# Five norms between products and a last one: by single token tile, with the next weights split earlier

## The chip, the cores and the metric

One core of one Trainium2 chip. The metric is the device time of one execution in microseconds (us), lower is better. Engines: TensorE (PE, matmuls and transposes), VectorE (DVE), ScalarE (ACT), GpSimd (POOL), and SyncE (SP), whose queue issues the DMAs.

## The reference

512 tokens of width 1024 pass through one block of a first kind and two layers of a second kind, all in 32-bit floating point. The parts between which the change works are chains of a product, a residual add, a norm over the width, and the next product:

```python
# first block
h = h + g1 * (merged @ w_out)
h = h + g2 * swiglu(modulate(rms_norm(h, w), sh2, sc2))     # w_gate, w_up, w_down
h = rms_norm(h, final_norm_w)
# each of two layers; ALPHA = 4 ** 0.25
h = layer_norm(ALPHA * h + g1 * (mix(h) @ w_out), ln1_g, ln1_b)
h = layer_norm(ALPHA * h + g2 * ffn(h), ln2_g, ln2_b)       # ffn: product, 3-tap conv, gate, product
```

`mix` joins three mixers; the third is an attention over three kinds of keys. All modulations (`sh`, `sc`, `g`) come from products of a condition vector with large matrices, which are computed beside the main chain.

## The kernel before, in words

**Products.** A 32-bit product is made of three matmuls on values split in a high and a low part (`mm3`, L389). A weight unit is a raw tile of 128x1024 (`wr`, 3 buffers), loaded on SP's queue (`wload`), multiplied by a gate row on GpSimd where the residual is gated (L370), copied by ScalarE into `wh` and subtracted by VectorE (or GpSimd, argument `e`) into `wl`, 3 buffers each (`feed`, L365). `gemm_R` (L1235) multiplies token tiles with such units: 4 token tiles of 128, two column halves `n` of 512, `nu` units per half, accumulators in PSUM banks by tag; `use` adds the result to the residual rows `x[t][n]`.

**Norms.** `boundary` (L1375) is the last product before a norm. It makes two passes, over token tiles 0 and 1, then 2 and 3, each over both column halves and two units per half. Three of the four units are kept for the second pass, and the unit (0, 0) is fed a second time. After a pass the two rows are normed (`rms_first`, `rms_last`, `ln_rows`), transposed by TensorE in four groups and *folded* (`fold_pair`, L1360): ScalarE applies scale and shift per feature, copies the high part, VectorE subtracts the low part; results are the tiles `hh`. Then `First` (L1344) computes the first three products of the next stage, in halves of 256 tokens, one product after the other; their weights come by `feed` with the subtract on GpSimd, inside `half(hh, 0)`. The affine step of the norm for the residual (`row_affine`, L1396) is done by GpSimd, a multiply and an add per half row. The places are called N1 (the first block's `w_out` into its gated product), N2 (its `w_down` into layer 0), N3 and N5 (the mixer of layer 0 and of layer 1 into the layer's `ffn`), N4 (layer 0's `ffn` into layer 1), N6 (the last norm, `last_rows`, L1658, whose rows go to the output).

**What comes before them.** In N1, N3 and N5 the product before has two parts: `gemm_R` over the first half of its inner width, then `boundary` over the second (L1451, L1638). In the layers the second half's inputs are the attention outputs `yc`; its last steps and `gemm_R` are interleaved on TensorE. After the last attention step the outputs of the other three token tiles are copied to high and low parts in tiles of the tag `act` (L1621 to L1625). In N1 the tag `f` (8 buffers) holds the tiles of the mixer merge (L1434 to L1444).

**What sets the order.** Each engine runs its instructions in one fixed order. A scheduler makes that order at build time: it takes what is ready in a modelled time, what stands under `tc.high_priority()` first and otherwise the earlier in the program. `tc.add_manual_dep(..., nosync)` puts one instruction behind another in this order without a wait on the chip. `note` (L253) uses it so that the first writes of tiles of one tag follow in program order:

```python
if key in last:
    tc.add_manual_dep(ins.ins, last[key].name, nosync, reason="slot order")
```

A tile is allocated when a buffer of its tag is free. `mm3` takes from the list `pace` an instruction that its first matmul must follow.

Of the kernel before, what the change touches and what calls it, by code (L numbers as in the profile page):

```python
# [16 lines left out]
P = 128  # L17
D = 1024
S = 512
# [195 lines left out]
def build(tc, I, out, at, dbg=None, stop=None):  # L215
# [132 lines left out]
    def tr(o, i):  # L348
        p = i.shape[0]
        note(o, PE.transpose(o, i, ident[:p, :p]))  # L350
# [14 lines left out]
    def feed(src, n=1024, soon=True, gate=None, e=V):  # L365
        with tc.high_priority() if soon else nullcontext():
            raw = wload(src, n)
            if gate is not None:
                r2 = raw.rearrange("p (k c) -> p k c", k=2)
                tt(r2, r2, gate[:, None, :].to_broadcast([P, 2, 512]), M_, e=G)  # L370
            hi = new(wp, [P, n], F32R, "wh", 3)
            lo = new(wp, [P, n], F32R, "wl", 3)
            if spare[0]:
                ts(hi, raw, 1.0, None, M_)
                tt(lo, raw, hi.bitcast(F32), S_, e=G)
            else:
                copy(hi, raw)
                tt(lo, raw, hi.bitcast(F32), S_, e=e)
        return hi, lo
# [49 lines left out]
    def cond_col(src, bias, cc, k0, plus, tag, as_row):  # L429
# [3 lines left out]
        sums = []  # L433
# [5 lines left out]
        for j in range(2):  # L439
            acc = W("cacc", NC[0])  # L440
            late(memset(acc, 0.0))
# [35 lines left out]
    def to_row(c, scale, name):  # L477
# [3 lines left out]
        t = new(qp, [NK, P], F32, "grow8", 1)  # L481
# [16 lines left out]
    cs = qp.tile([P, NK, 32], F32, name="cs")  # L498
# [56 lines left out]
    hp = hs.enter_context(tc.tile_pool(name="hp", bufs=1))  # L555
    hT = [[T([P, S], "act", 25, F32R, ap) for i in range(2)] for k in range(NK)]
# [664 lines left out]

    def fslot(dt=F32):
        return T([P, S], "f", 8, dt)
# [11 lines left out]
    def gemm_R(src, lhs, use, tags, toks=(0, 1, 2, 3), gate=None, kept=None):  # L1235


        nu = len(lhs) // 2
        units = [(n, u) for n in range(2) for u in range(nu)]
        if kept:  # L1240

            units = units[1:] + units[:1]
        left, b, again = [nu, nu], {}, dict(kept or {})
        for n, u in units:
            if n not in b:
                b[n] = [PS(g) for g in tags[n]]
            w_ = again.get((n, u)) or feed(src[n, u], gate=None if gate is None else gate[:, n * 512:(n + 1) * 512])
            if kept is not None and (n, u) != (0, 0):
                kept[n, u] = w_
            for i, t in enumerate(toks):  # L1250
                for kk in range(2):
                    mm3(b[n][i], lhs[2 * u + kk](t), [a[:, kk * 512:kk * 512 + 512] for a in w_],
                        left[n] == nu and kk == 0, left[n] == 1 and kk == 1)
            left[n] -= 1
            if not left[n]:
                for i, t in enumerate(toks):
                    use(t, n, b[n][i])
# [73 lines left out]
    def ln_rows(t):  # L1331
        e = SC if t == 1 else V
        mv, rs = ln_stats(t)
        if e is SC:
            mr = T([P, 1], "bmr", 2)
            ts(mr, mv[:, 0:1], rs, -1.0, M_, M_)
            for n in range(2):
                act(x[t][n], x[t][n], AF.Identity, bias=mr, scale=rs)
        else:
            for n in range(2):  # L1340
                ts(x[t][n], x[t][n], mv[:, 0:1], rs, S_, M_)
        return x[t]

    class First:  # L1344


        def __init__(self, srcs):
            self.srcs = srcs
# [11 lines left out]
    def fold_pair(hh, rows, s_, t_, i, tags):  # L1360

        o = slice(i * 256, i * 256 + 256)
        for kp in range(4):
            p = PS(tags[kp % len(tags)])
            for kk in range(2):
                k = 2 * kp + kk
                for t in range(2):
                    tr(p[:, (2 * kk + t) * P:(2 * kk + t + 1) * P], rows[t][k // 4][:, (k % 4) * P:(k % 4) * P + P])
# [6 lines left out]
    def boundary(src, lhs, gate, tags, norm, fs, tag, first, after=None, trs=(("sm",), ("tp", "o"))):  # L1375

        hh = [pair(tag) for _ in range(NK)] if fs else None
        fs = fs and fs()
        kept = {}
        for i in range(2):  # L1380
            gemm_R(src, lhs(i), plus, (tags[i][:2], tags[i][2:]), (2 * i, 2 * i + 1), gate, kept)
            if i and fs:
                first.half(hh, 0)
            if not fs:
                norm(i)
                continue
            rows = [norm(t) for t in (2 * i, 2 * i + 1)]
            fold_pair(hh, rows, *fs, i, trs[i])
# [7 lines left out]
    def row_affine(gr, br):  # L1396
        def use(t):
            for n in range(2):
                tt(x[t][n], x[t][n], gr[:, n * 512:(n + 1) * 512], M_, e=G)
                if br is not None:  # L1400
                    tt(x[t][n], x[t][n], br[:, n * 512:(n + 1) * 512], A_, e=G)
# [10 lines left out]
    def ffn(tile_, src, add0, add1, gate, cond, *rest, **kw):  # L1412

        for i, (a, b) in enumerate(((0, 12), (12, 18), (18, 22))):
# [5 lines left out]
            if i < 2:  # L1420
                gemm_R(src[:, a // 2:], by_tok(gu), add0 if i == 0 else add1, (B0, B1))
            else:
                return boundary(src[:, a // 2:], lambda i: by_tok(gu), gate, (B1, B0), *rest, **kw)
# [27 lines left out]
    gemm_R(I["w_out"], mg[:4], plus, (B0, B1), gate=g1)  # L1451
    tt(mod[-1, "sc2"], mod[-1, "sc2"], col("n2w"), M_)
    first = First([I["w_g"][0], I["w_u"][0], I["w_g"][1]])
    hh = boundary(I["w_out"][:, 2:], lambda i: mg[4:], g1, (B1, B0), rms_first,
# [22 lines left out]
    def mixer_first(l):  # L1477
        return First([I[f"w2c{l}"][i] for i in range(3)])
# [42 lines left out]
    def layer(l, hh, first):  # L1521
# [116 lines left out]
        gemm_R(I[f"w2o{l}"], by_tok(y2), plus_scaled, (B2, B2), gate=g1)  # L1638

        ycT = lambda i: [lambda t, k=k: tok(yc[t], k) for k in range(4)]  # L1640
        up = I[f"w2u{l}"]
        first = First([up[0], up[NF], up[1]])
        hh = boundary(I[f"w2o{l}"][:, 2:], ycT, g1, (B1, B0), ln_rows,
# [14 lines left out]
        def last_rows(i):  # L1658
            for t in (2 * i, 2 * i + 1):
                with tc.high_priority():  # L1660
                    mv, rs = ln_stats(t)
                for n in range(2):
                    c = slice(n * 512, (n + 1) * 512)
                    if i or n:
                        stt(x[t][n], x[t][n], mv[:, 0:1], rg[:, c], S_, M_)
                        stt(x[t][n], x[t][n], rs, rb[:, c], M_, A_)
                    else:
                        mr = T([P, 1], "bmr", 2)
                        ts(mr, mv[:, 0:1], rs, -1.0, M_, M_)
                        act(x[t][n], x[t][n], AF.Identity, bias=mr, scale=rs)  # L1670
                        tt(x[t][n], x[t][n], rg[:, c], M_, e=G)
                        tt(x[t][n], x[t][n], rb[:, c], A_, e=G)
                    load(out[t * P:(t + 1) * P, c], x[t][n])
# [278 lines left out]
```

## Time and profile before

| what | value |
|---|---|
| median of 3 runs | 2815.05 us (2814.28 to 2822.39) |
| profiled execution | 2818.97 us |
| its span, first to last instruction | 2816.9 us |
| instructions | 40296 |
| mean granted TensorE clock | 0.982 of full speed |

The profile shows one execution. "Busy" is the share of the span in which an engine runs an instruction. The granted clock is the mean over a stretch; TensorE runs at 1.2 or at 2.4 GHz, so 0.75 means half of the stretch at either. In a timeline a row gives the start, the time from the first to the last instruction of a run of equal ones, engine, line, operation, tiles, count, and in brackets the idle time before it and what ended it.

### The profile page before, as it was taken

The numbers are of one execution on the slowest core, as the hardware profiler recorded it, in microseconds if no ns is written. First come the engines' busy times: TensorE is split into PE (matmuls) and PEld (weight loads), VectorE is DVE, ScalarE is ACT, GpSimd is POOL, SyncE is SP. The second block draws the span as 40 slices with busy tenths as digits, with TensorE's granted clock in tenths as the row PEclk, the third lists the DMA queues.
The fourth block names the chain that finished last, engine by engine and source line by source line (L and its number), as shares of the span: only waits on it lengthen the run. The fifth ranks groups of instructions, "written<-read, shape, count | busy, mean of one in ns | idle before, by whom it ended". The sixth has DMA issues, their size and how long they took to land. (4 is left out here: it accounts for less than half of the span.)

```text
span 2816.9 us, 40296 instructions
## 1 busy us (share of the span) xinstructions
PE 2684.8 (95%) x15224; PEld 2218.8 (79%) x15224; DVE 1800.6 (64%) x2780; ACT 1371.6 (49%) x2516; POOL 1010.0 (36%) x678
## 2 busy tenths in 40 slices
PE   7999998999999989999999998999998999899997
PEld 4899987788786778787878877778787887788886
DVE  4777755867766464544556567775677666765557
ACT  5534435546555235535356654663635654443232
POOL 2333310322323045757521336674744223500013
PEclk9999999999999999999999999999999999999999
DMA  6222234434456835646322112654632211222222
GB/s 241 76 80 70 69 105 130 127 116 143 147 155 212 287 105 184 190 142 198 109 89 88 53 46 95 198 168 153 206 102 95 76 53 49 94 98 97 97 97 75
DMA packets 147187, 346.30 MB, mean 123 GB/s; under 512 B 13856, under 2 KB 48944, under 8 KB 143920
## 3 DMA queue, kind: packets, MB, share of 16 engines
q1 hardware_dynamic: 146992, 343.72, 38.2%
q8 instruction: 120, 1.97, 0.3%
q14 instruction: 75, 0.61, 0.1%
HBM read 326.73 MB, written 16.94 MB: 122 GB/s over the span
## 5 line engine op out<-in xcount | busy, mean ns | idle before, releaser
L312 PE MATMUL acc<-act,wh 128*128 128x512 f32 (+1 forms) x2944 | 869.2, 380 | 23.9 <-DVE act L300 13.7
L300 DVE TENSOR_TENSOR wl<-wr,wh 128x1024 fp32r<-128x1024 f32 (+1 forms) x329 | 468.8, 1427 | 424.8 <-ACT wh L297 412.1
L312 PEld LDWEIGHTS acc<-act,wh 128*128 128x128 f32 x2944 | 532.7, 192 | 142.0 <-issue 28.6
L297 ACT ACTIVATE wh<-wr 128x1024 fp32r<-128x1024 f32 (+1 forms) x344 | 359.2, 1046 | 526.6 <-PE sm L312 184.2
L312 PE MATMUL acc<-act,wl 128*128 128x512 f32 (+1 forms) x1472 | 528.0, 374 | 0.0
L312 PE MATMUL acc<-wh,act 128*128 128x256 f32 (+2 forms) x2312 | 498.6, 303 | 8.2 <-ACT cacc L291 4.4
L312 PEld LDWEIGHTS acc<-wh,act 128*128 128x128 f32 x2312 | 381.1, 192 | 29.1 <-ACT cacc L291 5.8
L312 PE MATMUL sm<-act,wh 128*128 128x512 f32 (+1 forms) x1232 | 369.5, 379 | 0.0
L300 POOL TENSOR_TENSOR cacc<-cacc,cw 128x512 f32<-128x512 f32 x192 | 311.7, 1626 | 140.0 <-DMA cacc<-in_b2a_dram 81.1
L312 PE MATMUL acc<-wl,act 128*128 128x256 f32 (+2 forms) x1156 | 347.8, 301 | 0.8 <-POOL wl L300 0.8
L312 PEld LDWEIGHTS acc<-act,wl 128*128 128x128 f32 x1472 | 274.1, 192 | 50.1 <-issue 6.9
L312 PEld LDWEIGHTS sm<-act,wh 128*128 128x128 f32 x1232 | 228.6, 189 | 44.0 <-issue 1.9
L312 PE MATMUL sm<-act,wl 128*128 128x512 f32 (+1 forms) x616 | 233.7, 379 | 0.7 <-DVE wl L300 0.7
L312 PEld LDWEIGHTS acc<-wl,act 128*128 128x128 f32 x1156 | 221.5, 192 | 9.9 <-POOL wl L300 1.0
L300 POOL TENSOR_TENSOR wl<-wr,wh 128x1024 fp32r<-128x1024 f32 x52 | 140.3, 2701 | 215.2 <-DVE wh L304 119.6
L297 ACT ACTIVATE cw<-cw,cc 128x512 f32<-128x512 f32 x192 | 136.1, 723 | 140.9 <-DMA cw<-in_w2a_dram 131.1
L300 POOL TENSOR_TENSOR wr<-wr,row 128x1024 f32<-128x1024 f32 x42 | 108.2, 2582 | 236.4 <-DMA f<-sp_gb 86.5
L300 POOL TENSOR_TENSOR x<-x,gx 128x512 f32<-128x512 f32 x32 | 48.3, 1535 | 297.2 <-DVE gx L300 297.2
L300 POOL TENSOR_TENSOR act<-act,wgt 128x512 f32<-128x512 f32 (+3 forms) x64 | 49.6, 795 | 252.4 <-DVE wgt L300 204.9
L312 PEld LDWEIGHTS sm<-act,wl 128*128 128x128 f32 x616 | 116.5, 189 | 22.9 <-DVE wl L300 1.5
L312 PE MATMUL sm<-wh,act 128*128 128x512 f32 (+1 forms) x392 | 123.5, 375 | 0.0
L1708 DVE CUSTOM_DVE_ANT_0 sm<-sm,K 128x512 f32<-128x512 f32 (+3 forms) x128 | 63.1, 498 | 84.1 <-PE sm L312 70.3
(447 smaller groups left out, 4595.2 us busy)
## 6 DMA issues: line engine op xcount, KB each, us to landing
cw<-in_w2a_dram SPq DMA_DIRECT2D x192, 256.0 KB
wr<-in_w2u_dram SPq DMA_DIRECT2D x88, 512.0 KB
wa<-in_wa_dram SPq DMA_DIRECT2D x24, 1024.0 KB
wr<-in_w2d_dram SPq DMA_DIRECT2D x46, 512.0 KB
wr<-in_w_bcx_dram SPq DMA_DIRECT2D x24, 512.0 KB
wr<-in_w2ab_dram SPq DMA_DIRECT2D x24, 512.0 KB
wr<-in_w_dn_dram SPq DMA_DIRECT2D x23, 512.0 KB
wr<-in_w_g_dram SPq DMA_DIRECT2D x22, 512.0 KB
```

The source lines that it names most:

```text
L297: note(o, SC.activation(o, i, AF.Copy, scale=scale))
L300: note(o, e.tensor_tensor(o, a, b, op=op))
L312: return note(o, PE.matmul(o, l, r, start=st, stop=sp))
L1708: m = V.tensor_tensor_reduce(p[:, :n], p[:, :n], con2("NU")[:, S - n:], 1.0, 3e38, A_, OP.min, mx)
```

## The change

Units of the product before a norm are all four kept, with four `wh` and `wl` buffers instead of three; nothing is fed twice. The product goes by single token tiles in a fixed order: first unit for tiles 0 and 1, second unit for tiles 0 and 1, then all of tile 2, all of tile 3; each group is put behind the one before. Each tile's row is normed when its product ends. The first pair's transposes stand behind tile 2, the second pair's behind the sixth of eight columns of the next products' first half, and use four PSUM tags each. `First` now goes column by column over its three products. It splits the first `n` of its sources ahead, into tiles of the tag `act` (n = 3: N3, N4, N5) or `f` (n = 2: N1, N2): between the two column halves of the product before (N1, N3, N5: `gemm_R` for the first inner half; N4: the `ffn`'s second product), in N2 inside `boundary`. These subtracts are VectorE's. Layer norms scale one half row on ScalarE and one on VectorE; the affine step moves from GpSimd to VectorE; the last norm is done tile by tile on VectorE. To make room, `cs` lies in a pool that is closed earlier, and two staging tiles of the condition rows are replaced by existing ones.

```diff
@@ wload / feed
-            hi = new(wp, [P, n], F32R, "wh", 3)
-            lo = new(wp, [P, n], F32R, "wl", 3)
+            hi = new(wp, [P, n], F32R, "wh", 4)
+            lo = new(wp, [P, n], F32R, "wl", 4)
@@ cond_col
-                t = new(qp, [1, 512], F32, "grow", 1)
-                copy(t, p[0:1])
-                load(d[:, 512 * j:512 * j + 512], t)
+                copy(accs[j][0:1], p[0:1])
+                load(d[:, 512 * j:512 * j + 512], accs[j][0:1])
@@ gemm_R
+        for n in range(2):
+            b = [PS(g) for g in tags[n]]
+            for u in range(nu):
+                w_ = feed(src[n, u], gate=None if gate is None else gate[:, n * 512:(n + 1) * 512])
+                for t in range(4):
+                    for kk in range(2):
+                        mm3(b[t], lhs[2 * u + kk](t), [a[:, kk * 512:kk * 512 + 512] for a in w_],
+                            u == 0 and kk == 0, u == nu - 1 and kk == 1)
+            for t in range(4):
+                use(t, n, b[t])
+            if mid and not n:
+                mid()
@@ ln_rows
+        act(x[t][1], x[t][1], AF.Identity, bias=mr, scale=rs)
+        ts(x[t][0], x[t][0], mv[:, 0:1], rs, S_, M_)
@@ First
+        def load(self):
+
+            self.w = []
+            with tc.high_priority():
+                for s in self.srcs[:self.n]:
+                    raw = wload(s)
+                    hl = [[self.slot(F32R) for _ in range(2)] for _ in range(2)]
+                    for j in range(2):
+                        split(raw[:, j * 512:j * 512 + 512], [a[j] for a in hl])
+                    self.w.append([Cat(a) for a in hl])
...
             if i == 0:
-                self.w = [feed(s, e=G) for s in self.srcs]
+                self.w.extend(feed(s) for s in self.srcs[self.n:])
                 self.p = [PS(g) for g in ("acc", "acc", "sm")]
-            for w_, p in zip(self.w, self.p):
-                for k in range(NK):
-                    o = slice(i * 256, i * 256 + 256)
+            o = slice(i * 256, i * 256 + 256)
+            for k in range(NK):
+                for w_, p in zip(self.w, self.p):
                     mm3(p[:, o], [a[:, k * P:(k + 1) * P] for a in w_], [a[:, o] for a in hh[k]],
                         k == 0 and i == 0, k == NK - 1 and i == 1)
+                if k == 5:
+                    end = recent[0]
+            return end
@@ boundary
+        w_ = [[feed(src[n, u], gate=None if gate is None else gate[:, n * 512:(n + 1) * 512]) for u in range(nu)]
+              for n in range(2)]
+        if fs and not first.w:
+            first.load()
+        tags = (("acc", "acc"), ("sm", "sm"), ("tp", "o"), ("ab", "o2"))
...
+        order = [(0, 0, 1), (1, 0, 1), (0, 1, nu), (1, 1, nu), (2, 0, nu), (3, 0, nu)]
+        for t, u0, u1 in order:
...
+            for n in range(2):
+                if behind:
+                    pace.append(behind)
...
+                behind = recent[0]
+                if u1 == nu:
+                    plus(t, n, p[t][n])
...
+            with tc.high_priority() if t == 3 else nullcontext():
+                rows.append(norm(t))
+            if t == 2:
+                fold_pair(hh, rows, *fs, 0, tags[1] + tags[0], behind)
+            elif t == 3:
+                pace.append(behind)
+                with tc.high_priority():
+                    fold_pair(hh, rows[2:], *fs, 1, tags[2] + tags[3], first.half(hh, 0))
@@ row_affine
-                tt(x[t][n], x[t][n], gr[:, n * 512:(n + 1) * 512], M_, e=G)
+                tt(x[t][n], x[t][n], gr[:, n * 512:(n + 1) * 512], M_)
@@ ffn
+                early = i == 1 and rest[3] and rest[3].n == 3
+                gemm_R(src[:, a // 2:], by_tok(gu), add0 if i == 0 else add1, (B0, B1), mid=rest[3].load if early else None)
@@ N1
+    first = First([I["w_g"][0], I["w_u"][0], I["w_g"][1]], fslot, 2)
+    gemm_R(I["w_out"], mg[:4], plus, (B0, B1), gate=g1, mid=first.load)
@@ N3 and N5, in layer
+        first = First([up[0], up[NF], up[1]], aslot, 3)
+        gemm_R(I[f"w2o{l}"], by_tok(y2), plus_scaled, (B2, B2), gate=g1, mid=first.load)
@@ last_rows
+        def last_rows(t):
+            mv, rs = ln_stats(t)
+            for n in range(2):
+                c = slice(n * 512, (n + 1) * 512)
+                stt(x[t][n], x[t][n], mv[:, 0:1], rg[:, c], S_, M_)
+                stt(x[t][n], x[t][n], rs, rb[:, c], M_, A_)
+                load(out[t * P:(t + 1) * P, c], x[t][n])
```

## Rows read from the trace of the kernel before

**Rows 1.** The page, part 1: busy time, share of the span and instructions.

```profile
PE 2684.8 (95%) x15224; PEld 2218.8 (79%) x15224; DVE 1800.6 (64%) x2780; ACT 1371.6 (49%) x2516; POOL 1010.0 (36%) x678
```

**Rows 2.** Windows N1 to N5: length, busy per engine (count), granted clock, DMA share, GB/s.

```profile
1009.20:1066.00 56.80, 48.51 (x275) 41.83 (x273) 28.98 (x51) 26.35 (x57) 15.66 (x10) 0.91 0.25 75
1398.70:1456.00 57.30, 52.42 (x296) 45.43 (x296) 32.82 (x53) 28.05 (x61) 24.94 (x17) 0.94 0.23 66
1702.00:1757.00 55.00, 46.63 (x268) 40.32 (x267) 40.19 (x51) 21.95 (x42) 37.13 (x27) 0.91 0.26 87
2094.50:2152.00 57.50, 49.07 (x284) 42.21 (x283) 46.77 (x64) 25.92 (x49) 36.48 (x25) 0.97 0.20 65
2400.00:2454.00 54.00, 45.75 (x246) 39.92 (x246) 37.43 (x49) 19.71 (x39) 34.42 (x26) 0.87 0.23 78
sum 280.60, PE 242.36 PEld 209.71 DVE 186.19 ACT 121.98 POOL 148.63; mean PE 48.47 PEld 41.94 DVE 37.24 ACT 24.40 POOL 29.73
```

**Rows 3.** TensorE's waits in N3: waited for, us in total, times, longest.

```profile
PE sm L350 <- ACT x L291: 4.0, 1, 4.0
```

**Rows 4.** Timelines: affine and fold in N3; fold in N1 (VectorE) and N4 (ScalarE).

```profile
1730.07 16.96 POOL L300 TENSOR_TENSOR x<-x,row 128x512 f32<-128x512 f32 x12
...
1732.96 15.02 DVE L300 TENSOR_TENSOR act<-gx,act 128x256 fp32r<-128x256 f32 x12
...
1056.28 1.43 DVE L300 TENSOR_TENSOR act<-gx,act 128x256 fp32r<-128x256 f32 x4 [6.21 <-ACT act L297]
...
2139.45 1.34 ACT L297 ACTIVATE act<-gx 128x256 fp32r<-128x256 f32 x4
```

**Rows 5.** Timeline of the end: last matmul, first and last VectorE work.

```profile
2791.78 0.39 PE L312 MATMUL acc<-wh,act 128*128 128x512 f32 x1
...
2792.20 1.28 DVE L300 TENSOR_TENSOR x<-x,acc 128x512 f32<-128x512 f32 x2 [4.25 <-PE acc L312]
...
2804.96 1.86 DVE L1323 BATCH_NORM_STATS2 bst<-x 128x6 f32<-128x512 f32 x3
...
2810.64 2.73 DVE L309 SCALAR_TENSOR_TENSOR x<-x,brs,row 128x512 f32<-128x512 f32 x4
```

**Rows 6.** The chain that ended last: 24 matmuls of 512 columns.

```profile
2478.60 5.49 PE sm L312 x24
```

**Rows 7.** Timeline, one unit's steps before N3: load, gate, copy, subtract.

```profile
1655.43 0.33 SPq L315 DMA_DIRECT2D wr<-in_w2o_dram  x1
...
1659.27 2.39 POOL L300 TENSOR_TENSOR wr<-wr,row 128x1024 f32<-128x1024 f32 x1 [7.02 <-DMA wr<-in_w2o_dram]
...
1693.86 1.06 ACT L297 ACTIVATE wh<-wr 128x1024 fp32r<-128x1024 f32 x1 [3.54 <-issue]
...
1699.85 1.22 DVE L300 TENSOR_TENSOR wl<-wr,wh 128x1024 fp32r<-128x1024 f32 x1 [0.45 <-ACT wh L297]
```

**Rows 8.** Timeline before N3: last attention scaling, copies of its output, first matmul of N3.

```profile
1689.70 0.76 POOL L300 TENSOR_TENSOR act<-act,wgt 128x128 f32<-128x128 f32 x2 [10.79 <-DVE wgt L300]
...
1700.20 1.67 ACT L297 ACTIVATE act<-act 128x512 fp32r<-128x512 f32 x3
...
1703.54 3.78 POOL L300 TENSOR_TENSOR act<-act,act 128x512 fp32r<-128x512 f32 x3
...
1700.36 0.50 PE L312 MATMUL acc<-wh,act 128*128 128x512 f32 x1 [1.10 <-ACT act L297]
```

**Rows 9.** Timeline before N1: the last merge tiles; the product's second column half starts.

```profile
998.67 0.68 DVE L300 TENSOR_TENSOR f<-f,f 128x512 f32<-128x512 f32 x1
...
1006.83 0.68 DVE L300 TENSOR_TENSOR act<-f,act 128x512 fp32r<-128x512 f32 x1
...
998.01 0.40 PE L312 MATMUL acc<-wh,act 128*128 128x512 f32 x1
```

**Rows 10.** Windows, the sum of 1750 to 1855; a two-input step in 2765 to 2792.

```profile
sum 105.00, PE 100.51 PEld 80.71 DVE 81.44 ACT 68.26 POOL 65.86; mean PE 33.50 PEld 26.90 DVE 27.14 ACT 22.75 POOL 21.95
...
2773.45 2.14 DVE L300 TENSOR_TENSOR f<-f,f 128x512 f32<-128x512 f32 x1
```

More of the change, by code (lines that the diff above doesn't have):

```diff
@@ L349, in tr @@
         p = i.shape[0]
[L350 removed]
+        return note(o, PE.transpose(o, i, ident[:p, :p]))
     def wload(src, n=1024):
@@ L432, in cond_col @@
         d = dp.tile([1, D], F32, name=tag + "d") if as_row else None
-        sums = []
+        sums, accs = [], []
         prev = recent[0]
@@ L1220, in f32slot, with aslot @@
         return T([P, S], "act", 25, F32, ap)
+    def aslot(dt):
+        return T([P, S], "act", 25, dt, ap)
     def fslot(dt=F32):
@@ L1233, in tok, with gemm_R @@
         return [b[:, t * P:(t + 1) * P] for b in a]
-    def gemm_R(src, lhs, use, tags, toks=(0, 1, 2, 3), gate=None, kept=None):
+    def gemm_R(src, lhs, use, tags, gate=None, mid=None):
         nu = len(lhs) // 2
[L1239 to L1257, printed above, removed]
+        for n in range(2):
[10 more added lines that the diff above has]
+                mid()
     def by_tok(pairs):
@@ L1331, in ln_rows @@
     def ln_rows(t):
-        e = SC if t == 1 else V
         mv, rs = ln_stats(t)
[L1334 to L1341, printed above, removed]
-        return x[t]
-    class First:
-        def __init__(self, srcs):
-            self.srcs = srcs
+        mr = T([P, 1], "bmr", 2)
@@ L1373, in fold_pair, with boundary @@
                 split(u[:, c], [a[:, o] for a in hh[k]])
-    def boundary(src, lhs, gate, tags, norm, fs, tag, first, after=None, trs=(("sm",), ("tp", "o"))):
+    def boundary(src, lhs, gate, norm, fs, tag, first, after=None):
         hh = [pair(tag) for _ in range(NK)] if fs else None
[L1378 to L1383, printed above, removed]
+        if fs:
+            fs = fs()
+        nu = len(lhs(0)) // 2
+        w_ = [[feed(src[n, u], gate=None if gate is None else gate[:, n * 512:(n + 1) * 512]) for u in range(nu)]
[3 more added lines that the diff above has]
+        tags = (("acc", "acc"), ("sm", "sm"), ("tp", "o"), ("ab", "o2"))
+        behind, rows = None, []
+        p = [[PS(g) for g in r] for r in tags[:2]]
+        order = [(0, 0, 1), (1, 0, 1), (0, 1, nu), (1, 1, nu), (2, 0, nu), (3, 0, nu)]
+        for t, u0, u1 in order:
+            k_ = lhs(t // 2)
+            if t > 1:
+                p.append([PS(g) for g in tags[t]])
+            for n in range(2):
+                if behind:
+                    pace.append(behind)
+                for u in range(u0, u1):
+                    for kk in range(2):
+                        mm3(p[t][n], k_[2 * u + kk](t), [a[:, kk * 512:kk * 512 + 512] for a in w_[n][u]],
+                            u == 0 and kk == 0, u == nu - 1 and kk == 1)
+                behind = recent[0]
+                if u1 == nu:
+                    plus(t, n, p[t][n])
+            if u1 < nu:
+                continue
             if not fs:
-                norm(i)
+                norm(t)
                 continue
-            rows = [norm(t) for t in (2 * i, 2 * i + 1)]
-            fold_pair(hh, rows, *fs, i, trs[i])
+            with tc.high_priority() if t == 3 else nullcontext():
[6 more added lines that the diff above has]
+                    fold_pair(hh, rows[2:], *fs, 1, tags[2] + tags[3], first.half(hh, 0))
         if fs:
@@ L1477, in mixer_first @@
     def mixer_first(l):
-        return First([I[f"w2c{l}"][i] for i in range(3)])
+        srcs = [I[f"w2c{l}"][i] for i in range(3)]
+        return First(srcs, aslot, 3) if l else First(srcs, fslot, 2)
     nxt = mixer_first(0)
```

52 lines of the change are left out of this document (21 added, 31 removed).

## The prediction

> **What bounds the kernel now.** I read the busy table first: TensorE is busy 2684.8 of 2816.9 us, VectorE 64%, ScalarE 49%, GpSimd 36% [rows 1]. The change removes no matmul, so it can only win back time in which TensorE stands still or runs at its lower clock. Next the table by stretches, over the five places N1 to N5 where one product ends in a norm and feeds the next: 280.6 us, of which TensorE is busy 242.4 [rows 2]. So 38.2 us are idle, 4.9 to 8.4 us in each, and the granted clock is 0.87 to 0.97 there, where undisturbed stretches show 1.00. A mean of c over a stretch of w us is 1.2 GHz for 2(1-c)w of it, which costs (1-c)w where TensorE works: 5.1 + 3.4 + 5.0 + 1.7 + 7.0 = 22.2, and 19 after multiplying by the busy share of 0.86. The five places lose about 57 us together. Then the waits and the timeline of N3. The longest wait is for normed rows, 4.0 us [rows 3]. While GpSimd does 12 affine steps (16.96 us), VectorE's 12 small subtracts of the fold take 15.02 us, 1.25 each; four of the same kind in N1, where GpSimd does no affine, take 1.43, 0.36 each [rows 4]. TensorE waits there for VectorE, and VectorE for GpSimd. Last the end of the kernel: the last matmul ends at 2792.2, the last VectorE work at 2813.4, the span at 2816.9 [rows 5]. That tail is 24.7 us.
>
> **The sum's base.** The profiled execution took 2818.97 us, 2.1 more than its span; the median of the runs shown is 2815.05. I sum against 2819.0 and take 3.9 off at the end.
>
> **Passes by token tile, fold by pairs, affine on VectorE.** One tile's products are 24 matmuls, 5.5 us by the chain [rows 6], so when the last tile ends, the first pair's rows are normed and its 16 transposes done. Behind the last tile stand 72 matmuls of 256 columns (the work of 36 of 512: 8.2 us) that need the first pair only, and the second pair's transposes come after three quarters of them, 6.2 us. The last tile's norm needs less: an add 0.64, statistics 0.62, the root through GpSimd, one scale, some 4 us. The fold then costs ScalarE about 0.85 us for each of 8 columns (four copies 1.34, and as much for the affine step) [rows 4] while TensorE, now column by column over three products, uses 1.03 us for each. So TensorE finds each column ready, and the 57 us (57.5 before rounding) shrink to small misfits of an order fixed beforehand; I leave 2 us in each place: **-47.5 us**. Bounds: 0.5 left in each (-55), or half of it kept because ScalarE is late (-29). The affine's 16 multiplies and adds per norm now cost VectorE 16 x 0.68 = 11 us, after the fold, when it has little to do; it saves as much in subtracts. The first unit is no longer loaded, gated and split a second time: 512 KB, 2.4 us of GpSimd, 1.1 of ScalarE and 1.2 of VectorE per place, all beside TensorE: 0. The condition rows that now pass through the accumulator hold it a few us longer; GpSimd's sums for them lie beside 60 us of products: 0.
>
> **The last norm.** VectorE's work per tile is two adds 1.28, two statistics 1.24, four fused steps 2.73 [rows 5], 5.25 us, 21 for four. The first tile's first half is complete 6.9 us into the pass of 22 us, so VectorE ends 6.1 us after TensorE, 7.6 with a stop of 1.5 (an estimate) for the last root, where it is 21.2 today: **-13.6 us**. Bounds: -16 (no stop), -7 (the first tiles start a tile late).
>
> **The next weights inside the preceding product.** Here a wait is added. In program order the next three sources are loaded and split between the two column halves of the product before the norm. The raw tiles have three buffers and are taken in order, so the second half's first unit can be loaded only when the first next source has been split, and its splits write tiles of the tag `act`, whose first writes are chained in program order (`note`). In the two layers the tiles before them are the copies of the attention output; today these come at 1700.2 on ScalarE and from 1703.5 on GpSimd [rows 8], after the last attention step, although three of the four outputs were ready long before. What is queued behind: the unit's DMA on SP, its gate on GpSimd, its copy and subtract: 3.84 + 2.39 + 1.06 + 1.22 = 8.5 us from load to use [rows 7]. Today this path runs ahead, and the second half fills TensorE during the last attention steps.
>
> When does it end? GpSimd's last scaling ends at 1690.5 [rows 8]. Without the second half between them, transposes, copy and product follow in some 2 us, the copies of the output end at 1694.1, the first source's split (two copies, two subtracts, 2.2 us) at 1696.3. Plus 8.5: the second half starts at 1704.8, and needs 11.0 us and some 2 us at the lower clock after 13 idle us: 1717.8, where the next product starts at 1700.4 today. That is 17.4 us per layer, **+34.8 us**. Bounds: 0, if the splits turn out to be early, and 30.6 per layer, if the copies stay where they are (GpSimd ends them at 1707.3; + 2.2 + 8.5 + 13 = 1731). I take the value between, since the steps in front of the copies lose the matmuls that delay them.
>
> In N1 the splits go to the 8 tiles of tag `f`, all in use by the last two tiles of the mixer merge: one frees them at about 999, the other after 1007.5 [rows 9]. The second half's second unit then comes at 1000.5 + 8.5 = 1009 for a need at 998 + 5.5: 5.5 late. The norm's own units follow the second split at about 1017.4 for 1014.5: 2.9. The fixed order asks for the third unit 1.4 us after the first, and GpSimd gates one per 2.4: 3.4. Together **+11 us**, bounds 0 and 15. In N2 the split stays in the norm, and in N4 the product has 16 us per half for a path without a gate: 0 for both; if the 24 or so live `act` tiles hold it up, some 5 us.
>
> **Sum.** -47.5 - 13.6 + 34.8 + 11 = -15.3, against 2819.0: 2803.7, against the median **2800 us**.
>
> **Rivals.** *The splits are early* and hold nothing up: -61.1 us, 2754. For it: a raw tile of this product is loaded at 1655.4 today, 45 us before the next product starts [rows 7, 8], and ScalarE has gaps. Against it: the chained copies have the same gaps in front of them and still come last [rows 8].
>
> *The wait is whole* (slower): the second half of both layer products waits behind the next weights for as long as the copies are late today: 61.2 + 11 - 61.1 = +11, 2826. Place: between 1686 and 1731 and the same 30 us in layer 1. It decides from 25 us per layer on, where the two waits eat the 61.1 less 11. For it: an engine takes its work in a fixed order, and the copies on GpSimd come 3 us after ScalarE's. Against: nothing else would stand on TensorE by then.
>
> *VectorE becomes the bound behind the norms.* In the first 105 us after N3 it is busy 81.4 us and TensorE already idles 4.5; a two-input step that takes 0.68 elsewhere [rows 9] took 2.14 beside a GpSimd gate [rows 10]. If the 16 affine steps fall there, they cost up to 16 x 1.46 = 23 us, all the room there is; 5 us of it per place for three places on TensorE: 2815. The Trainium skill, SBUF — State Buffer, Practical consequences, says that a VectorE instruction with two SBUF inputs contends with a GpSimd instruction that reads SBUF, and that the second to start is fully blocked. By that rule moving the affine off GpSimd only turns round who waits as long as GpSimd sums the conditions there. The trace agrees on the price; but without its affine GpSimd has nothing but roots to do until the fold ends, where I expect the steps.
>
> **Chances.** Forecast 0.47 (own range 2785 to 2816: the stages' gain 29 to 55 is the wide term, the two waits lean against it), early splits 0.26, whole wait 0.19, VectorE 0.08. A measurement of this kernel can tell about 0.3%, 8.4 us: faster is below 2806.6, slower above 2823.5. Faster: 0.33 of the forecast, 0.26, 0.01, 0.02 = 0.62. Same: 0.11 + 0.05 + 0.03 = 0.19. Slower: 0.03 + 0.13 + 0.03 = 0.19. The range 2757 to 2826 leaves out half of the early case and half of the whole wait, 0.2.
>
> **What would show it.** Right: subtracts of the fold at 0.36 us without an affine on GpSimd beside them; idle of TensorE in N2 and N4 near 2 us and clock 1.00; the last VectorE work 8 us after the last matmul; in both layers a gap of 10 us or more ahead of the second column half, with raw loads waiting on SP until the next source's first subtract; in N1 waits for `wl` or `wh`. Wrong: TensorE dense through 1690 to 1720, which makes it 2754 to 2770; or subtracts and affine steps above 1 us, or transposes of the second pair that wait for ScalarE, which leaves the loss in place.

## The result, and the profile after

The changed kernel takes 2834.86 us (median of 4 runs, 2833.57 to 2835.57), the kernel before 2814.66 beside it: a ratio of **1.0062, 95% interval [1.0048, 1.0075]**, slower by some 17 us, 0.6%. I had forecast 2800, within 2757 to 2826; the time lies above the range. The profiled execution after has a span of 2831.8 us, 14.9 more than before.

The busy table of the changed kernel's page answers to [rows 1]:

```profile
PE 2675.2 (94%) x15224; PEld 2211.0 (78%) x15224; DVE 1787.9 (63%) x2863; ACT 1364.5 (48%) x2527; POOL 873.7 (31%) x597
```

The windows N1 to N5 answer to [rows 2], with the same columns. Each begins and ends with the same TensorE instruction, by its number in the sequence of 15224, as the one of before.

```profile
1008.22:1063.89 55.67, 47.30 (x275) 40.65 (x274) 26.88 (x49) 25.14 (x56) 9.06 (x7) 0.94 0.25 78
1395.60:1448.90 53.30, 50.27 (x297) 44.39 (x295) 33.13 (x67) 27.68 (x63) 2.20 (x4) 0.97 0.26 80
1709.98:1764.61 54.63, 46.27 (x267) 40.91 (x266) 35.53 (x71) 19.77 (x40) 2.26 (x4) 0.91 0.29 95
2109.94:2162.49 52.55, 47.96 (x284) 42.21 (x283) 40.79 (x80) 23.78 (x47) 2.20 (x4) 0.97 0.16 51
2424.99:2475.07 50.08, 41.73 (x247) 36.52 (x246) 35.54 (x71) 19.67 (x40) 2.26 (x4) 0.93 0.28 88
sum 266.23, PE 233.53 PEld 204.68 DVE 171.88 ACT 116.05 POOL 17.98; mean PE 46.71 PEld 40.94 DVE 34.38 ACT 23.21 POOL 3.60
```

GpSimd's 148.63 us in these stretches fell to 17.98: the affine, the second feeding and the subtracts of the next weights are gone from it. But the stretches are only 14.4 us shorter (280.60 to 266.23), where I wanted 47.5. TensorE still idles 32.7 us in them, and N3 is as long as before, 54.6 for 55.0.

**Where the time went.** I took the start of the n-th TensorE instruction in either trace and followed the difference, after less before, from mark to mark (marks in the time of before; us; the kernels e1 to e12 are those of the next section).

| stretch | after | e1 | e2 | e3 | e6 | e8 | e9 | e12 |
|---|---|---|---|---|---|---|---|---|
| N1, 990 to 1100 | 0.0 | -0.1 | -5.5 | -0.3 | -4.6 | -3.0 | -4.4 | -4.5 |
| N2, 1395 to 1480 | -4.5 | -4.1 | -5.7 | -8.8 | -4.5 | -8.8 | -9.2 | -9.0 |
| ahead of N3, 1680 to 1702 | **+19.1** | +2.0 | +1.0 | +19.2 | +1.0 | +1.2 | +0.9 | +2.0 |
| N3, 1702 to 1760 | -1.1 | +0.1 | +0.2 | -7.9 | -8.5 | -7.0 | -6.2 | -8.9 |
| behind N3, 1760 to 1800 | -1.0 | -1.0 | -1.0 | +6.3 | -0.4 | +0.4 | -0.7 | -1.0 |
| tiles and product, 1800 to 2000 | +3.0 | +3.1 | +3.3 | +0.9 | +8.4 | +2.6 | +9.6 | +1.9 |
| product ahead of N4, 2000 to 2040 | +6.7 | +6.7 | 0.0 | +6.0 | 0.0 | 0.0 | 0.0 | 0.0 |
| N4, 2040 to 2170 | -4.6 | -4.7 | +2.6 | -10.3 | +1.9 | -3.4 | -3.5 | -4.0 |
| ahead of N5, 2380 to 2400 | **+16.6** | 0.0 | -1.1 | +17.2 | -0.4 | -1.1 | -0.2 | 0.0 |
| N5, 2400 to 2460 | -4.7 | -1.7 | -1.2 | -9.8 | -9.1 | -10.1 | -10.1 | -10.3 |
| behind N5, 2460 to 2500 | 0.0 | 0.0 | +0.1 | +5.6 | 0.0 | 0.0 | 0.0 | 0.0 |

Behind the last matmul another 5.6 us are won. The attention steps just ahead of the two waits are quicker in the changed kernel: taken from 1550 to 1702 and from 2350 to 2400 its difference to before grows by 14.8 and 12.3 only, in e1 by +0.7 and -1.0. So the waits cost some 27 us net. e1 and e5 have the same instructions up to the first layer, yet their profiled executions stand 8.2 us apart at 990; so I read differences between near marks, and whole kernels by their ratios.

**The next weights hold the second half.** The waits of TensorE in the changed kernel from 1680 to 1765 (columns as in [rows 3]):

```profile
PE acc L312 <- ACT wh L297: 13.3, 1, 13.3
PE sm L312 <- DVE act L300: 6.0, 2, 4.4
PE acc L312 <- DVE x L309: 2.0, 2, 1.7
```

Its timeline around the longest of them:

```profile
1679.95 1.66 ACT L297 ACTIVATE act<-act 128x512 fp32r<-128x512 f32 x3
1681.51 3.22 ACT L297 ACTIVATE act<-wr 128x512 fp32r<-128x512 f32 x6
...
1682.16 5.61 DVE L300 TENSOR_TENSOR act<-wr,act 128x512 fp32r<-128x512 f32 x6 [1.38 <-ACT act L297]
...
1685.39 14.55 SPq L315 DMA_DIRECT2D wr<-in_w2o_dram  x6
...
1689.24 7.99 POOL L300 TENSOR_TENSOR wr<-wr,row 128x1024 f32<-128x1024 f32 x3 [4.43 <-issue]
...
1691.62 1.06 ACT L297 ACTIVATE wh<-wr 128x1024 fp32r<-128x1024 f32 x1 [6.89 <-POOL wr L300]
```

And the window of it up to TensorE's return (columns as in [rows 2]):

```profile
1680.00:1692.73 12.73, 0.00 (x1) 0.01 (x1) 6.33 (x8) 5.78 (x11) 7.65 (x5) 0.50 0.37 124
```

The copies of the attention output end at 1681.5, the next sources are split right behind them, and only with the first raw tile free is the second half's first unit loaded, at 1685.39; gate and copy follow, and TensorE goes on at 1692.73. The window shows it idle from 1680, at a granted clock of 0.50, 1.2 GHz. [rows 7, 8] are the same steps before.

**VectorE's order holds the fold.** The timeline of VectorE in N3 from the third tile's rows to the second of the first pair's eight subtracts, and the weights' subtract behind it:

```profile
1728.12 1.22 DVE L300 TENSOR_TENSOR wl<-wr,wh 128x1024 fp32r<-128x1024 f32 x1
1729.25 2.49 DVE L300 TENSOR_TENSOR x<-x,row 128x512 f32<-128x512 f32 x4
1731.66 0.68 DVE L300 TENSOR_TENSOR x<-x,ab 128x512 f32<-128x512 f32 x1
1732.26 1.28 DVE L300 TENSOR_TENSOR x<-x,row 128x512 f32<-128x512 f32 x2
1733.46 0.41 DVE L300 TENSOR_TENSOR act<-gx,act 128x256 fp32r<-128x256 f32 x1
1733.80 0.68 DVE L300 TENSOR_TENSOR x<-x,row 128x512 f32<-128x512 f32 x1
1734.40 1.21 DVE L300 TENSOR_TENSOR wl<-wr,wh 128x1024 fp32r<-128x1024 f32 x1
1735.53 0.68 DVE L300 TENSOR_TENSOR x<-x,row 128x512 f32<-128x512 f32 x1
...
1737.34 1.20 DVE L300 TENSOR_TENSOR wl<-wr,wh 128x1024 fp32r<-128x1024 f32 x1
1738.46 0.41 DVE L300 TENSOR_TENSOR act<-gx,act 128x256 fp32r<-128x256 f32 x1
1738.80 1.22 DVE L300 TENSOR_TENSOR wl<-wr,wh 128x1024 fp32r<-128x1024 f32 x1
```

TensorE's rows there, each with its wait:

```profile
1733.93 0.62 PE L312 MATMUL sm<-act,act 128*128 128x256 f32 x3 [1.63 <-DVE act L300]
...
1738.93 1.01 PE L312 MATMUL sm<-act,act 128*128 128x256 f32 x3 [4.38 <-DVE act L300]
```

The subtracts of the fold take 0.41 us now, where 12 took 15.02 beside GpSimd's affine [rows 4]: that part came true. But around the first two of them stand 8 affine steps (`x<-x,row`, 5.1 us) and 4 subtracts of weights for later tiles (4.9 us). In the kernel before, such weights' subtracts came behind the fold, the first at 1755.84. That the scheduler took all these as ready in its modelled time, ahead of the fold, fits its rule; the modelled times are not on record. TensorE waits 1.6 us for the first column and 4.4 us for the second (together the 6.0 of the second wait above), and the granted clock of N3 is 0.91, as before.

### The profile page after: what moved, and what is told of

Read it like the earlier page. It is cut to its first block, busy times and chain, and to the rows that moved or that the text cites. A ratio compares the mean times of both kernels' runs of the same rounds, so it can differ in the third digit from the quotient of the medians.

```text
span 2831.8 us, 40251 instructions
## 1 busy us (share of the span) xinstructions
PE 2675.2 (94%) x15224; PEld 2211.0 (78%) x15224; DVE 1787.9 (63%) x2863; ACT 1364.5 (48%) x2527; POOL 873.7 (31%) x597
## 4 chain that ended last, share of the span: by engine, by line
PE 68%; DVE 9%; ACT 7%; DMA 6%; POOL 5%; issue 4%; SPq 0%; POOLq 0%; DVEq 0%; ACTq 0%
PE acc L312 36%; PE sm L312 18%; PE o L312 6%; POOL cacc L300 5%; PE ab L312 2%; DVE wl L300 2%; PE tp L312 2%; ACT wh L297 1%; DMA cw<-in_w2a_dram 1%; DVE x L300 1%; PE sm L350 1%; PE dtr L312 1%; PE tp L350 1%; DMA rf<-sp_A 1%; DMA evl<-sp_oa 1%
## 5 line engine op out<-in xcount | busy, mean ns | idle before, releaser
L312 PE MATMUL acc<-act,wh 128*128 128x512 f32 (+1 forms) x2624 | 793.5, 388 | 8.4 <-ACT act L297 3.5
L297 ACT ACTIVATE wh<-wr 128x1024 fp32r<-128x1024 f32 (+1 forms) x325 | 338.7, 1045 | 475.7 <-PE sm L312 201.1
L312 PEld LDWEIGHTS acc<-act,wh 128*128 128x128 f32 x2624 | 473.9, 190 | 119.7 <-issue 23.6
L312 PE MATMUL acc<-wh,act 128*128 128x256 f32 (+2 forms) x2312 | 499.0, 303 | 12.7 <-ACT cacc L291 4.4
L312 PE MATMUL acc<-act,wl 128*128 128x512 f32 (+1 forms) x1312 | 481.5, 382 | 0.0
L312 PE MATMUL sm<-act,wh 128*128 128x512 f32 (+1 forms) x1136 | 351.9, 386 | 0.7 <-DVE act L300 0.7
L312 PEld LDWEIGHTS acc<-act,wl 128*128 128x128 f32 x1312 | 240.7, 190 | 50.4 <-issue 7.2
L312 PEld LDWEIGHTS sm<-act,wh 128*128 128x128 f32 x1136 | 212.5, 189 | 45.4 <-issue 2.6
L312 PE MATMUL sm<-act,wl 128*128 128x512 f32 (+1 forms) x568 | 219.5, 386 | 0.1
L300 POOL TENSOR_TENSOR wl<-wr,wh 128x1024 fp32r<-128x1024 f32 x37 | 102.7, 2777 | 181.0 <-DVE wh L304 125.3
L300 POOL TENSOR_TENSOR wr<-wr,row 128x1024 f32<-128x1024 f32 x36 | 94.9, 2651 | 186.1 <-DMA f<-sp_yb 81.0
```

Source lines behind the costliest of these rows:

```text
L297: note(o, SC.activation(o, i, AF.Copy, scale=scale))
L300: note(o, e.tensor_tensor(o, a, b, op=op))
L312: return note(o, PE.matmul(o, l, r, start=st, stop=sp))
```

## The experiments

All twelve were timed in five rounds beside the kernel before. `mid` is the loading between the two column halves.

**e1, layers without mid.**

```diff
-        gemm_R(I[f"w2o{l}"], by_tok(y2), plus_scaled, (B2, B2), gate=g1, mid=first.load)
+        gemm_R(I[f"w2o{l}"], by_tok(y2), plus_scaled, (B2, B2), gate=g1)
```

> Edit: in the two layers the three next sources are loaded and split inside the norm boundary again, not between the two column halves of the product before it; all else as changed. Theory (the next weights' wait is what stops TensorE ahead of the second half): the stops of 13.3 and 12.8 us there go, with the low clock after them, so 13 to 14 us in each layer come back: about 27 us, a span near 2805, ratio 0.997 to the kernel before. Rival 1 (the stop only moves): the split then stands in the norm, the first products wait for it as long, ratio 1.006 as now. Rival 2 (half): the stop goes, but 6 subtracts of 1.22 us, 7.3 us, stand on VectorE ahead of the norm and the fold in each layer, so half of it comes back: ratio 1.002.

Measured: 0.9975 [0.9964, 0.9985]. The two places ahead of N3 and N5 fall from +19.1 and +16.6 to +2.0 and 0.0; of the 35.7 us N3 and N5 give some 4 back, and the attention steps ahead lose what they had won by it. The difference of the ratios, 0.0087, is 24.5 us, near the 27 net less 4. This undoing alone takes the kernel below the one before: the theory, not the rivals.

**e2, no mid at all.** The edit of e1, and the same in N1 and in the `ffn` (`early`).

> Edit: as the run before, and in N1 and ahead of N4 too the next sources are loaded in the boundary. Theory: the product ahead of N4 lost 6.8 us by the alignment of the two traces, and N1 gained nothing where 5 to 10 us of its 10.7 were to be won; both come back, 12 us on top of 27, ratio 0.993. Rival: in N1 and N4 the early split cost nothing (what is lost there is the order in the boundary), ratio 0.997 as without them.

Measured: 0.9951 [0.9937, 0.9965]. Half of the theory holds. N1 gains 5.5 us; but what the product ahead of N4 wins, 6.7, N4 itself loses, -4.6 to +2.6, since the split now stands in it. In the changed kernel the early split showed there as five subtracts at 1.6 us each beside GpSimd's sums, in the timelines of VectorE and GpSimd:

```profile
2038.53 8.04 DVE L300 TENSOR_TENSOR act<-wr,act 128x512 fp32r<-128x512 f32 x5 [0.39 <-ACT act L297]
...
2038.06 6.39 POOL L300 TENSOR_TENSOR cacc<-cacc,cw 128x512 f32<-128x512 f32 x4 [0.46 <-ACT cw L297]
```

and as a wait of TensorE for late weights, from 2030 to 2070:

```profile
PE acc L312 <- DVE wl L300: 2.7, 1, 2.7
```

**e3, affine behind the fold.** A scheduling order without a wait on the chip:

```diff
+            hold[0] = recent[0]            # last subtract of the second pair's fold
             first.half(hh, 1)
...
-                tt(x[t][n], x[t][n], gr[:, n * 512:(n + 1) * 512], M_)
+                tt(x[t][n], x[t][n], gr[:, n * 512:(n + 1) * 512], M_, hold=hold[0])
```

> Edit: the changed kernel with the affine steps on VectorE ordered behind the last subtract of the second pair's fold, nothing else. Theory (VectorE's order holds the fold): at N3 some 15 us of VectorE's work lie between the first pair's rows and its last subtract, 5.4 of it 8 affine steps; the stop of 4.4 us before the first column shrinks below 2, and each of N2 to N5 wins 2 to 4 us: 12 us, ratio 1.002. Rival 1 (ScalarE's copies of the next weights hold the fold, not VectorE): nothing moves, 1.006. Rival 2: the later affine delays the subtracts of the following weights: 1.008.

Measured: 1.0014 [1.0005, 1.0023]. The fold is early now; the 4.4 us were the second column's, and that wait is gone, while the first column's is 1.7 us for 1.6: N2 to N5 gain 4.3, 6.8, 5.7 and 5.1 us on the changed kernel in their stretches. Right behind N3 and N5 6.3 and 5.6 are given back, which I had not expected. VectorE's timeline behind the fold of N3:

```profile
1751.34 9.71 DVE L300 TENSOR_TENSOR x<-x,row 128x512 f32<-128x512 f32 x16
```

and TensorE's wait from 1750 to 1800:

```profile
PE acc L314 <- DVE f L311: 3.4, 1, 3.4
```

The 16 steps in one block (0.61 us each) now stand ahead of the `ffn`'s first gating steps `f`, which free the accumulators.

**e4, affine and following weights behind the fold.** As e3, and in `feed` the copy `hi` gets the same `hold`.

> Edit: as the run before, and the split of the weights of the tiles after the first three (a copy on ScalarE, a subtract on VectorE) is ordered behind the fold too. Theory (the affine and the early weights together hold the fold): the stops before the first column fall below 1 us, 4 to 5 us in each of N2 to N5 and some 3 in N1: about 20 us, ratio 0.999. Rival 1: the weights then come late for the fourth product, with a new stop of 3 to 5 us in each place: 1.004 to 1.008. Rival 2: VectorE's order is not what costs, 1.006.

Measured: 1.0044 [1.003, 1.0057]: the first rival's time, but not its wait, as the late weights cost only 1.2 us. N3 and N5 win still more in the stretch (-11.1, -12.7) and give 9.4 and 8.5 back. It is the wait for `f` behind N3 that is longer:

```profile
PE acc L314 <- DVE f L311: 6.1, 1, 6.1
```

VectorE's row of windows for the stretch N3:

```profile
1715.78:1758.20 42.42, 41.34 (x267) 37.34 (x266) 26.24 (x59) 19.42 (x41) 2.22 (x4) 1.00 0.10 30
```

In the stretch itself VectorE is busy 26.24 of 42.42 us; behind the fold, from 1753.7 to 1778, it runs almost without a gap. What is moved out of the fold's way must be moved to where there is room.

**e5, affine spread, with mid.**

```diff
                 gu.append(tile_(j))
+                if drip and j > 0:
+                    f, t, n = drip.pop(0)
+                    hold[0] = recent[0]
+                    f(t, (n,))
```

> Edit: the changed kernel; in the two layers (N3 and N5) the affine's 16 steps on VectorE are handed out two at a time, each pair behind the last step of one of the ffn's tiles 1 to 8; N2 and N4 as changed. Theory (VectorE is nearly full behind the norm, so the affine must neither stand ahead of the fold nor ahead of the first tiles): the fold is as early as where the affine stood behind it (8.4 us by the alignment at N3, some 4 at N5), and the 6.2 and 5.6 us given back right behind it stay won: 11 to 16 us off the changed kernel, ratio 0.9985 to 1.0005 less what N4 loses: 1.000. Rival (VectorE is full through the tiles as well, the price follows the steps wherever they go): ratio 1.003 to 1.006.

Measured: 1.0039 [1.0024, 1.0054], within the rival's range. By the trace it holds in one layer only: N3 and N5 gain 6.1 and 5.0 without giving back right behind, but from 1800 to 2000 layer 0 loses 8.0 for 3.0: its tiles, too, seem to have no room, as GpSimd's sums of the conditions run there (rows at e6). Which wait carries the loss was not followed.

**e6, no mid and affine spread.**

> Edit: the next sources loaded in the boundary everywhere, and the affine of N3 and N5 spread over tiles 1 to 8. Theory: the two gains add, as they lie in different stretches: 0.9951 less 11 to 16 us, ratio 0.9905, and the stop of 4.4 us before the first column at N3 falls to 2 or less. Rival (with the split inside the boundary VectorE is as late without the affine, since 6 subtracts of 1.22 us stand there): 0.995, no gain.

Measured: 0.993 [0.9917, 0.9942]. Between theory and rival: the gains add, but so does e5's loss in layer 0 (+8.4 from 1800 to 2000). At N3 the second column's wait of 4.4 us is gone and the first column's is left:

```profile
PE sm L314 <- DVE act L300: 1.7, 1, 1.7
```

In layer 0 an affine step takes 0.68 us where GpSimd is idle and up to 1.78 beside its sums:

```profile
1788.86 0.68 DVE L300 TENSOR_TENSOR x<-x,row 128x512 f32<-128x512 f32 x1
...
1802.63 1.78 DVE L300 TENSOR_TENSOR x<-x,row 128x512 f32<-128x512 f32 x1
...
1795.20 16.02 POOL L300 TENSOR_TENSOR cacc<-cacc,cw 128x512 f32<-128x512 f32 x9 [9.93 <-DVE f L311]
```

**e7, no mid, affine on GpSimd** (`e=G` in `row_affine`, as before the change).

> Edit: the next sources loaded in the boundary everywhere, and the affine of N2 to N5 on GpSimd as in the kernel before. Theory (GpSimd's steps beside the fold make VectorE's subtracts 1.25 us instead of 0.36, so the affine on GpSimd holds the fold as much as on VectorE): 8 subtracts x 0.9 = 7 us of VectorE per place in place of 5.4 of affine: ratio 0.995 to 0.998, no faster than with the affine on VectorE. Rival (GpSimd's affine runs after the first pair's fold, and VectorE is freed of 11 us): 0.990.

Measured: 0.995 [0.9937, 0.9962], as e2 with the affine on VectorE: moving the affine off GpSimd neither won nor lost by itself. At N3 TensorE waits as long for the fold, 4.6 us, now because the subtracts run beside GpSimd's steps (1.26 to 1.48 us each, not 0.41):

```profile
1711.96 1.26 DVE L300 TENSOR_TENSOR act<-gx,act 128x256 fp32r<-128x256 f32 x1
...
1721.21 2.91 DVE L300 TENSOR_TENSOR act<-gx,act 128x256 fp32r<-128x256 f32 x2
...
1709.45 14.39 POOL L300 TENSOR_TENSOR x<-x,row 128x512 f32<-128x512 f32 x8 [0.79 <-PE sm L350]
```

The sum of its five stretches, bounded by the same instructions:

```profile
sum 268.36, PE 238.33 PEld 206.21 DVE 190.55 ACT 121.92 POOL 99.19; mean PE 47.67 PEld 41.24 DVE 38.11 ACT 24.38 POOL 19.84
```

**e8, no affine.** The steps after N2 to N5 are left out.

> Edit: the next sources loaded in the boundary everywhere, and the affine of the rows after N2 to N5 left out altogether (so the rows that the next blocks add to lack their norm's scale and shift; the products are fed as before). It tells the most that any place for the affine can win. Theory: N3 and N5 win 6 to 8 us each, N2 and N4 up to 2: ratio 0.988 to 0.990, within 2 us of the spread one. Rival (what holds the fold is the weights' split on ScalarE and VectorE, not the affine): 0.993 to 0.995.

Measured: 0.9859 [0.9842, 0.9875], more than the theory gave. Against e2 that is 0.0092, 26 us, for at most 56 steps (8 for N2, 16 each for N3 to N5) that take 0.61 us alone, 34 us. So three quarters of what the affine takes on VectorE reach the time, when it stands where the change put it. The spread of e6 was not within 2 us of this, as I had thought, but 20 us above.

**e9, affine by place.** N2 and N4: three column halves behind each of the next mixer's first products; N3: two behind each unit of the first `ffn` product; N5: behind the tiles.

> Edit: the next sources loaded in the boundary everywhere; the affine steps each behind a step with room: after N2 and N4 three at a time (columns) behind the next mixer's first products, after N3 two at a time behind the units of the first ffn product (its tiles before have GpSimd's sums of the conditions beside them), after N5 behind the tiles as before. Theory: the last run's ceiling without any affine is 0.986 and the spread one stands at 0.993; of that 20 us, 5 were given back by the affine between the tiles of layer 0, 4 each lie at N2 and N4: 13 us, ratio 0.9885. Rival (11 us of steps per norm cost what they cost wherever they stand): 0.992 to 0.994.

Measured: 0.9883 [0.9866, 0.99]; the theory to 0.0002, but by luck, as its parts differ: N2 and N4 win 4.7 and 5.4 us on e6, and the 5 us of layer 0 do not come (+9.6 from 1800 to 2000, +8.4 in e6). One stop is left there, 6.2 us of the +9.6 with the clock after it. The timeline of VectorE and GpSimd there:

```profile
1874.60 13.71 DVE L300 TENSOR_TENSOR x<-x,row 128x512 f32<-128x512 f32 x10
...
1875.91 11.85 POOL L300 TENSOR_TENSOR cacc<-cacc,cw 128x512 f32<-128x512 f32 x7 [6.78 <-ACT cw L297]
```

and TensorE's only wait from 1870 to 1900, for the weights behind the ten steps:

```profile
PE tp L314 <- DVE wl L300: 4.5, 1, 4.5
```

**e10, copies after.** In the changed kernel the loop that copies the attention output (`for t in (3, 2, 1)`) moves behind `gemm_R`.

> Edit: the changed kernel; in the layers the copies of the attention output are written after the gated product in program order, so that the first writes of the next sources' tiles are not chained behind them. Theory (my prediction's: the chain of first writes sets when the splits start): they start behind the last exponential, at 1676.6 in place of 1681.5, the stop of 13.3 us at N3 falls to about 8.4, as at N5: 10 us, ratio 1.0027. Rival (the chain is not what counts; raw tiles or the engines' queues are): the stop stays between 12 and 14, ratio 1.005 to 1.007.

Measured: 1.006 [1.0045, 1.0075]. The ratio is the rival's, the trace the theory's: the splits now come ahead of the copies, the first unit is loaded directly after, and the stop is 9.7 us instead of 13.3. What it wins is lost behind: GpSimd's copies now stand between the gates of the second half's units, as the timeline shows (ScalarE, SP, GpSimd):

```profile
1674.77 3.22 ACT L297 ACTIVATE act<-wr 128x512 fp32r<-128x512 f32 x6
1677.88 1.66 ACT L297 ACTIVATE act<-act 128x512 fp32r<-128x512 f32 x3
...
1676.82 20.26 SPq L315 DMA_DIRECT2D wr<-in_w2o_dram  x6
...
1682.79 3.52 POOL L300 TENSOR_TENSOR act<-act,act 128x512 fp32r<-128x512 f32 x2
```

and TensorE's longest wait from 1650 to 1775:

```profile
PE acc L312 <- ACT wh L297: 9.7, 1, 9.7
```

**e11, one source.**

```diff
-        first = First([up[0], up[NF], up[1]], aslot, 3)
+        first = First([up[0], up[NF], up[1]], aslot, 1)
```

> Edit: the changed kernel; in the layers one of the three next sources is loaded and split inside the product, two are fed in the norm. Theory (three raw tiles, all held by the next sources, are what keeps the second half's units from being loaded): two raw tiles are then free for the second half's two units, the stop goes (under 2 us), the two later sources cost 2 to 4 us at the first columns: ratio 0.998 to 1.001. Rival (the splits stand ahead of the second half's copies in ScalarE's and VectorE's queues whatever the raw tiles do): the stop stays above 10 us, ratio 1.004 or more.

Measured: 0.9964 [0.995, 0.9977]. Ahead of N3 and N5 stand +2.0 and 0.0, as without mid, and no wait from 1655 to 1720 is over 1.1 us. With two raw tiles free the second half's units come past the next source: they are loaded 15 us before ScalarE copies it, in the timelines of SP and ScalarE:

```profile
1679.76 2.49 SPq L315 DMA_DIRECT2D wr<-in_w2o_dram  x2
...
1694.45 1.14 ACT L297 ACTIVATE act<-wr 128x512 fp32r<-128x512 f32 x2
```

So what carries the wait is that the next sources hold all three raw tiles; the chain of first writes only sets when it ends (e10).

**e12, affine one half row by unit.** As e9, with `drop(1)` behind each unit after N3, first column half first.

> Edit: the run before that placed the affine by room (0.9883); after N3 one row half (two steps) behind each unit of the first ffn product, first column half first, in place of four steps behind each. Theory: there ten affine steps in a row took 13.7 us beside GpSimd's sums (1.37 each), and the subtract of the next unit's weights behind them came 4.5 us late, the one stop over 2 us between 1780 and 1990; with two or six steps in a row it goes, 6 us with the clock after it: ratio 0.986 to 0.987, the level without any affine (0.9859). Rival (the contended steps cost TensorE as much in pieces): 0.988 as before.

Measured: **0.9865 [0.9848, 0.9882]**, 2778.25 us: the fastest that leaves nothing out, 1.35% below the kernel before and at the level without any affine. From 1800 to 2000 +1.9 us are left. The sum of its five stretches, bounded by the same instructions:

```profile
sum 241.98, PE 228.04 PEld 200.61 DVE 145.32 ACT 119.65 POOL 13.34; mean PE 45.61 PEld 40.12 DVE 29.06 ACT 23.93 POOL 2.67
```

So the change without the early split, and with the affine out of the way, is worth 38.6 us in the five stretches (280.6 to 242.0). That is not the order by token tiles and pairs alone: with the affine on GpSimd as before, e7, the stretches are 268.4, so the new order and what goes with it give 12 us, and the affine's place behind it the other 26. No run moves the affine out of the stretches in the kernel before, so what its place would win in the old order is open.

## Why the prediction was wrong, step by step

**Five stages, -47.5: this is the step that failed.** They gave -14.4 with N1's wait among it, some -20 without. The text placed the affine "after the fold, when it has little to do", and left 2 us in each place. Neither the order nor the room was as said. The order put half of the steps ahead of the first pair's fold, and behind the fold VectorE has the first tiles' gating, which e3 showed by 6.3 and 5.6 us. I had costed 11 us of a moved step at nothing behind a cover that was thin by my own row: [rows 10] gave VectorE 81.4 of 105 us there. The weights' subtracts for later tiles, which I did not count, stood in front of the fold as well. With the affine out of the way the stretches give 38.6 of the 47.5 (e12), so the time was there; but only 12 of it came from the order while the affine ran in the stretch (e7). ScalarE's 0.85 us per column is not in [rows 4] either, where two steps of 1.34 / 4 are 0.67.

**The layers' wait, +34.8: right in its mechanism, 7.7 us too large.** The stops of 13.3 and 12.8 us, SP's raw loads behind the first source's subtract and the chain behind the copies came as written, some 12 us earlier in time, as the whole kernel was 11 ahead there. From mark to mark they show as +19.1 and +16.6, but with the attention steps ahead, which run without the second half between them, the two places lost 14.8 and 12.3 us, against 17.4 each. The 2 us at the lower clock stood in the sum without a row; after the stop, from 1692.73 to 1709.98, the granted clock was 0.90, which by the way of reckoning in the prediction is 1.7 us. To an early end (0.26) and a whole wait (0.19) I had given nearly half of the chance, and the middle was right.

**N1, +11: too much.** With and without mid N1 stands at 0.0 and -5.5, so 5.5 us. (The three parts of the sum, 5.5, 2.9 and 3.4, are 11.8.)

**N2 and N4, 0 for the early split: right in sum only.** The product ahead of N4 lost 6.7 us, and N4 won 7.2 by it (-4.6 against +2.6 in e2).

**The last norm, -13.6: a row misread.** The tail shrank by 5.6 us. I had taken the matmul at 2791.78 [rows 5] for the last; most of the second pass, with the unit that is fed a second time, comes after it. The last rows of TensorE before, then of TensorE and VectorE after:

```profile
2801.30 0.39 PE L312 MATMUL o<-wh,act 128*128 128x512 f32 x1
```

```profile
2821.86 0.39 PE L312 MATMUL o<-wh,act 128*128 128x512 f32 x1
...
2827.45 1.41 DVE L309 SCALAR_TENSOR_TENSOR x<-x,brs,row 128x512 f32<-128x512 f32 x2
```

The tail before was 2816.9 - 2801.7 = 15.2 us, not 24.7, and is 9.6 now. VectorE ends 6.6 us after TensorE, near the 7.6 I gave (6.9 + 21 - 22 is 5.9 and not 6.1, so 7.4); the tail I started from was 9.5 us too long.

**Put together.** The stages fell short by 27.6 us (-47.5 to -19.9, in which N4's gain is counted), the tail by 8.0, and the product ahead of N4 cost 6.7; N1 gave 5.5 back and the layers' wait 7.7. That turns the sum of -15.3 into +13.8, and the two spans differ by 14.9; the forecast of 2800 becomes 2829. The last 6 us to 2834.9 lie mostly outside these two profiles, as the medians differ by 20.2. The rival with VectorE, to which I gave 0.08, named the engine but not the place: it put the price behind the norm, beside GpSimd's sums, where the changed kernel loses nothing (-1.0 and 0.0 behind N3 and N5). The forecast set it aside because GpSimd would be idle until the fold ends, but the steps need no contention to stand in the way. Where they do run beside GpSimd's sums, they cost twice: 13.71 / 10 = 1.37 us in e9, 0.61 in e3. The Trainium skill, SBUF — State Buffer, Practical consequences, says that a VectorE instruction with two SBUF inputs contends with a GpSimd instruction that reads SBUF; the rows agree. e7 shows the affine to cost as much on either engine, but not by that rule alone: on GpSimd it slows the fold's subtracts, on VectorE it stands in front of them at its own 0.6 to 0.7 us a step.

## What to carry to other kernels

A step moved to another engine "for later" lands where the scheduler puts it, which may be in front of the very work that the move was to free; write down, for each us of it, the rows between which it will stand, and tie it there with an ordering if they matter. A prefetch put between two halves of a product takes its buffers in turn with the second half: count the raw tiles first, since with one source in three (e11) the wait was gone, and with three it cost 24.5 us (e1), more than the five stretches won in the changed kernel. And find the last instruction of an engine by asking for the last rows of that engine alone.

## What had not been expected of the hardware

The same two-input step of VectorE over 128x512 took 0.61 us in a block of 16 with GpSimd idle, and 1.37 in a row of 10 beside seven sums on GpSimd that took 1.69 each (11.85 / 7). And e1 and e5, equal up to there, reach the 5546th TensorE instruction at 991.0 and 982.8 us: a difference of a few us between two whole spans says little.
